# First load swapped, section entered and left through GpSimd, in a batched product of two transposed matrices

## The chip, the cores and the metric

One core of one Trainium2 chip. The metric is the time of one execution in microseconds, on the device. Most executions of a kernel agree within 0.3%. Verdicts use a border of 2%: faster, same, slower. A core has TensorE (PE; PEld is its weight load), VectorE (DVE), ScalarE (ACT), GpSimd (POOL) and SyncE (SP), and 16 transfer (DMA) engines. A span in a profile is shorter than the time of the same execution: 123.0 us against 124.78 us.

## The reference

```python
batch, m, k, n = 16, 512, 512, 512
a: (batch, k, m) float32      b: (batch, n, k) float32
out = np.matmul(a.transpose(0, 2, 1), b.transpose(0, 2, 1))   # float32
```

Both operands come transposed. 16.8 MB of a and of b are read and 16.8 MB written, 50.33 MB in all.

## The kernel before

The batches are loaded whole. Four buffers hold one batch of a each (1.05 MB, 8 KB in each of 128 partitions), three hold a pair of batches of b each (2.10 MB, 16 KB a partition). ScalarE casts a to bf16. VectorE casts b, TensorE turns it against the identity, VectorE copies it back, then TensorE multiplies. SyncE issues all loads from a single queue, in a fixed order, and the last stores; ScalarE issues the first five stores.

```python
with tc.tile_critical():                       # the section; SyncE opens it
    ...
    def run_sp(sp):
        for i in range(B):
            for p in ([0] if i == 0 else [(i + 1) // 2] if i % 2 and i + 1 < B else []):
                if p >= PAIRS:
                    sp.wait_ge(turned, p - PAIRS + 1)
                sp.dma_start(b_sb[p % PAIRS][:], b_v[p]).then_inc(b_in[p % PAIRS], 16)
            s, use = i % LOADS, i // LOADS
            if use:
                sp.wait_ge(summed, MO * (i - LOADS) + 1)    # the buffer has been used
            ...
            sp.dma_start(a_sb[s][:], a_v[i]).then_inc(a_in[s], 16)
        ...                                    # the last stores
        sp.reg_mov(all_stored, 16 * STORED)
    def run_act(act):
        cast_a(act, 0)
        for i in range(B - 1):
            cast_a(act, i + 1)
            copy_out(act, i, slice(2, 4), oa_go)
            j, odd = divmod(i - LAG, 2)
            if odd and 0 <= j < H - TAIL:
                store(act, j)
    ...
nc.sync.wait_ge(stored, nc.sync.snap(all_stored))   # behind the section
```

The first seven loads (10.5 MB) need no wait. They go out at once in the order b0, a0, b1, a1, a2, b2, a3, where b0 is the first pair.

Of the kernel before, what the change touches and what calls it, by code (L numbers as in the profile page):

```python
# [11 lines left out]
def kernel(  # L12
# [6 lines left out]
    nc = tc.nc  # L19
# [15 lines left out]
    a_v = a.rearrange("b (ki ko) m -> b ki ko m", ko=KO)  # L35
# [9 lines left out]
    STORED = H - (H - OUTS) + 1  # L45

    stored = tc.alloc_semaphore("stored")

    all_stored = nc.sync.alloc_register("all_stored")

    with tc.tile_critical():  # L51
        sb = lambda name, shape, dt: ctx.enter_context(nc.sbuf_tensor(name, shape, dt))
        ps = lambda name, shape, dt: ctx.enter_context(nc.psum_tensor(name, shape, dt))
        sem = tc.alloc_semaphore
        a_sb = [sb(f"a_sb{s}", [P, KO, M], f32) for s in range(LOADS)]
# [12 lines left out]
        a_in = [sem(f"a_in{s}") for s in range(LOADS)]  # L68
# [14 lines left out]
        def store(eng, j, part=slice(0, 2)):  # L83


            eng.dma_start(
                out_v[2 * j + part.start:2 * j + part.stop].rearrange("b p mo n -> p b mo n"),
                o_sb[j % OUTS][:, part],
            ).then_inc(o_out[j % OUTS] if j + OUTS < H else stored, 16)

        def run_sp(sp):
            for i in range(B):

                for p in ([0] if i == 0 else [(i + 1) // 2] if i % 2 and i + 1 < B else []):
                    if p >= PAIRS:
# [4 lines that stand above are left out]
                    sp.wait_ge(summed, MO * (i - LOADS) + 1)  # L100
                if i % 2 == 0 and i // 2 >= OUTS:

                    sp.wait_ge(o_out[i // 2 % OUTS], 16 * (i // 2 // OUTS))
                sp.dma_start(a_sb[s][:], a_v[i]).then_inc(a_in[s], 16)

            for j in range(H - TAIL, H - 1):
                sp.wait_ge(summed, MO * (2 * j + 2) + 3)
                store(sp, j)

            sp.wait_ge(summed, MO * (B - 1) + 1)  # L110
            sp.wait_ge(half_go, 1)
            store(sp, H - 1, slice(0, 1))
            sp.wait_ge(last_go, 3)
            store(sp, H - 1, slice(1, 2))
            sp.reg_mov(all_stored, 16 * STORED)

        def run_pool(pool):
            pool.sem_inc(od_go, 1)
            pool.sem_inc(oa_go, 1)
            pool.memset(identity[:], 0.0).then_inc(id_go, 1)  # L120
            pool.wait_ge(id_go, 1)
            pool.affine_select(  # L122
                out=identity[:],
                in_=identity[:],
                compare_op=mybir.AluOpType.not_equal,
                fill=1.0,
                base=0,
                pattern=[[-1, P]],
                channel_multiplier=1,
            ).then_inc(id_go, 1)  # L130

        def cast_a(act, i):
            s = i % LOADS
            act.wait_ge(a_in[s], 16 * (i // LOADS + 1))
            act.copy(a_bf[i % 2][:], a_sb[s][:]).then_inc(ac_go, 1)  # L135
# [56 lines left out]
        def run_pe(pe):  # L192
# [41 lines left out]
            with pe.Fori(0, H) as _i:  # L234
# [6 lines left out]
                half(1, 1)  # L241

        run_sp(nc.sync)
        run_pool(nc.gpsimd)
        run_dve(nc.vector)
        run_act(nc.scalar)
        run_pe(nc.tensor)


    nc.sync.wait_ge(stored, nc.sync.snap(all_stored))  # L250


# [28 lines left out]
```

## Time and profile before

| | before |
|---|---|
| time, median of 3 runs | 124.80 us (124.68 to 124.91) |
| span of the profile | 123.0 us |
| moved | 50.33 MB, 409 GB/s over the span, 427 in its middle |
| first bytes move, last bytes moved | 1.96 us, 121.46 us |
| first product begins | 15.55 us |
| last store asked for, landed | 116.54 us, 121.93 us |

### The profile page before, as it was taken

The numbers are of one execution on the slowest core, as the hardware profiler recorded it, in microseconds if no ns is written. First come the engines' busy times: TensorE is split into PE (matmuls) and PEld (weight loads), VectorE is DVE, ScalarE is ACT, GpSimd is POOL, SyncE is SP. The second block draws the span as 40 slices with busy tenths as digits, with TensorE's granted clock in tenths as the row PEclk, the third lists the DMA queues.
The fourth block names the chain that finished last, engine by engine and source line by source line (L and its number), as shares of the span: only waits on it lengthen the run. The fifth ranks groups of instructions, "written<-read, shape, count | busy, mean of one in ns | idle before, by whom it ended". The sixth has DMA issues, their size and how long they took to land. (4 is left out here: it accounts for less than half of the span.)

```text
span 123.0 us, 1086 instructions
## 1 busy us (share of the span) xinstructions
PE 86.1 (70%) x400; PEld 49.7 (40%) x400; DVE 56.4 (46%) x48; ACT 46.8 (38%) x34; POOL 0.7 (1%) x6
## 2 busy tenths in 40 slices
PE   0006497997999799779930799965992679979600
PEld 0006344642755464346410546442640526437300
DVE  0016368478295755917039107780719306171200
ACT  4003209537717903176300950329230490750300
POOL 2000000000000000000000000000000000000000
PEclk9999999999999999999995557999999558999995
DMA  4999999999999999999999999999999999999992
GB/s 91 394 400 458 400 424 456 429 394 456 426 397 448 434 376 432 426 440 440 416 421 429 458 408 418 429 426 437 453 397 432 426 426 426 429 426 426 429 424 115
DMA packets 5648, 50.33 MB, mean 409 GB/s; under 512 B 528, under 2 KB 528, under 8 KB 528
## 3 DMA queue, kind: packets, MB, share of 16 engines
q1 hardware_dynamic: 4288, 39.85, 77.2%
q10 hardware_dynamic: 1360, 10.49, 20.1%
HBM read 33.55 MB, written 16.78 MB: 409 GB/s over the span
## 5 line engine op out<-in xcount | busy, mean ns | idle before, releaser
L219 PE MATMUL o_ps<-bt_sb,a_bf 128*128 128x512 bf16 x256 | 65.1, 403 | 7.1 <-PEq L194 6.6
L135 ACT CAST a_bf<-a_sb 128x2048 bf16<-128x2048 f32 x16 | 30.4, 1900 | 40.8 <-DMA a_sb<-in_a_dram 40.8
L219 PEld LDWEIGHTS o_ps<-bt_sb,a_bf 128*128 128x128 bf16 x256 | 28.5, 115 | 37.5 <-issue 15.0
L205 PE MATMUL bt_ps<-identity,b_bf 128*128 128x128 f32 x144 | 24.3, 323 | 22.7 <-PEq L194 22.7
L144 DVE COPY o_sb<-o_ps 128x1024 f32<-128x1024 f32 x16 | 19.6, 1224 | 35.8 <-PE o_ps L219 35.8
L205 PEld LDWEIGHTS bt_ps<-identity,b_bf 128*128 128x128 f32 x144 | 22.2, 212 | 28.2 <-issue 27.2
L152 DVE CAST b_bf<-b_sb 128x2048 bf16<-128x2048 f32 x16 | 19.5, 1221 | 19.1 <-DMA b_sb<-in_b_dram 19.1
L144 ACT COPY o_sb<-o_ps 128x1024 f32<-128x1024 f32 (+1 forms) x17 | 16.4, 962 | 28.0 <-PE o_ps L219 28.0
L161 DVE COPY bt_sb<-bt_ps 128x1024 f32<-128x1024 f32 x16 | 19.5, 1216 | 3.1 <-PE bt_ps L205 3.1
L135 ACT ACT_TABLE_LOAD x1 | 1.3, 1283 | 0.9 <-SPq L51 0.9
L122 POOL TENSOR_SCALAR_AFFINE_SELECT identity<-identity 128x128 f32<-128x128 f32 x1 | 0.3, 294 | 0.2 <-POOL identity L120 0.2
L120 POOL MEMSET identity<- 128x128 f32 x1 | 0.2, 205 | 0.7 <-SPq L51 0.7
L265 POOL MEMSET const-bfloat16-1.0<- 128x1 bf16 x1 | 0.1, 102 | 0.0
L265 POOL MEMSET const-uint8-127<- 128x1 uint8 x1 | 0.1, 102 | 0.0
L265 POOL MEMSET const-float32-0.0<- 128x1 f32 x1 | 0.1, 99 | 0.2 <-issue 0.2
L265 POOL MEMSET const-float32-1.0<- 128x1 f32 x1 | 0.1, 99 | 0.0
## 6 DMA issues: line engine op xcount, KB each, us to landing
b_sb<-in_b_dram SPq DMA_DIRECT2D x8, 2048.0 KB, 20.4
a_sb<-in_a_dram SPq DMA_DIRECT2D x16, 1024.0 KB, 17.5
out_dram<-o_sb ACTq DMA_DIRECT2D x5, 2048.0 KB, 15.2
out_dram<-o_sb SPq DMA_DIRECT2D x2, 2048.0 KB, 13.6
out_dram<-o_sb SPq DMA_DIRECT2D x2, 1024.0 KB, 6.3
```

The source lines that it names most:

```text
L120: pool.memset(identity[:], 0.0).then_inc(id_go, 1)
L122: pool.affine_select(out=identity[:], in_=identity[:], compare_op=mybir.AluOpType.not_equal, fill=1.0, base=0, pattern=[[-1, P]], channel_ ...
L135: act.copy(a_bf[i % 2][:], a_sb[s][:]).then_inc(ac_go, 1)
L144: copy(o_sb[i // 2 % OUTS][:, i % 2, rm, :], o_ps[h][:, p, :]).then_inc(go, 1)
L152: dve.tensor_copy(b_bf[:, r, :], b_sb[p % PAIRS][:, r, :]).then_inc(bc_go, n)
L161: dve.tensor_copy(bt_sb[g][:].rearrange("p j (ni r) -> p j ni r", r=NR), bt_ps[:].rearrange("p j r (g ni) -> p g j ni r", g=2)[:, g],).the ...
L205: last = pe.transpose(bt_ps[:, j, r, :], w[:, r, j, :], identity[:])
L219: last = pe.matmul(o_ps[h][:, q, :], a_r[:, rk, 2 * h + q, :], bt_h[:, rk // 2, rk % 2, :], start=(rk == 0), stop=(rk == KO - 1),)
L265: nc = _bacc.Bacc("TRN2", target_bir_lowering=False, num_devices=1)
```

## The change

The intent was to have the first a in hand early, and to start and end a little sooner by letting GpSimd, which already gathers the engines at the barriers of the program, open the section and wait for the last stores.

```diff
-    all_stored = nc.sync.alloc_register("all_stored")
-    with tc.tile_critical():
+    all_stored = nc.gpsimd.alloc_register("all_stored")
+    with tc.tile_critical(sync_engine=nc.gpsimd.engine):
 ...
         def run_sp(sp):
             for i in range(B):
+                if i == 0:
+                    sp.dma_start(a_sb[0][:], a_v[0]).then_inc(a_in[0], 16)
 ...
-                sp.dma_start(a_sb[s][:], a_v[i]).then_inc(a_in[s], 16)
+                if i:
+                    sp.dma_start(a_sb[s][:], a_v[i]).then_inc(a_in[s], 16)
 ...
-            sp.reg_mov(all_stored, 16 * STORED)
         def run_pool(pool):
 ...
+            pool.reg_mov(all_stored, 16 * STORED)
 ...
-    nc.sync.wait_ge(stored, nc.sync.snap(all_stored))
+    nc.gpsimd.wait_ge(stored, nc.gpsimd.snap(all_stored))
```

## The prediction

> **What bounds the kernel now.** I read the page's slices first, because they show which row is full all the time.
>
> ```profile
> PE   0006497997999799779930799965992679979600
> ...
> DMA  4999999999999999999999999999999999999992
> GB/s 91 394 400 458 400 424 456 429 394 456 426 397 448 434 376 432 426 440 440 416 421 429 458 408 418 429 426 437 453 397 432 426 426 426 429 426 426 429 424 115
> DMA packets 5648, 50.33 MB, mean 409 GB/s; under 512 B 528, under 2 KB 528, under 8 KB 528
> ```
>
> The transfer engines stand at 9 in 38 of 40 slices; only the first slice (3.1 us) and the last have room. TensorE falls to 0 and 3 in the middle of the run while transfers stay full, so it waits for data. 50.33 MB is the least that can be moved: each input read once, the output written once. At the 427 GB/s of the middle of the run that alone takes 50.33 / 0.427 = 117.9 us of the 123.0 us span. About 5 us are left at the two edges, and the change can gain only there.
>
> Second view: the windows table at the edges. Columns: window and length; busy time of PE, weight load, DVE, ACT, POOL with counts; granted clock; transfer share; GB/s.
>
> ```profile
> 1.40:1.80 0.40, 0.00 (x0) 0.00 (x0) 0.00 (x0) 0.40 (x1) 0.26 (x1) 1.00 0.00 0
> 1.80:2.00 0.20, 0.00 (x0) 0.00 (x0) 0.00 (x0) 0.20 (x1) 0.03 (x1) 1.00 1.34 328
> ...
> 120.00:120.50 0.50, 0.00 (x0) 0.00 (x0) 0.00 (x0) 0.00 (x0) 0.00 (x0) 0.50 1.00 426
> 120.50:121.00 0.50, 0.00 (x0) 0.00 (x0) 0.00 (x0) 0.00 (x0) 0.00 (x0) 0.50 0.40 164
> 121.00:121.50 0.50, 0.00 (x0) 0.00 (x0) 0.00 (x0) 0.00 (x0) 0.00 (x0) 0.50 0.08 33
> 121.50:122.00 0.50, 0.00 (x0) 0.00 (x0) 0.00 (x0) 0.00 (x0) 0.00 (x0) 0.50 0.00 0
> ```
>
> Data begin to move just under 2.0 us and stop just under 121.5 us. So the span is about 2.0 us of entry, 119.5 us of transfer (a ramp up and down included) and 1.5 us of ending. Third view: the timeline of the first microseconds, which shows the entry and what the order of the loads sets.
>
> ```profile
> 0.90 1.28 ACT L135 ACT_TABLE_LOAD   x1 [0.90 <-SPq L51]
> 0.95 0.39 SPq L97 DMA_DIRECT2D b_sb<-in_b_dram  x1
> ...
> 1.39 0.42 SPq L104 DMA_DIRECT2D a_sb<-in_a_dram  x1
> ...
> 8.81 2.36 DVE L152 CAST b_bf<-b_sb 128x2048 bf16<-128x2048 f32 x2 [8.81 <-DMA b_sb<-in_b_dram]
> 10.15 3.29 PEld L205 LDWEIGHTS bt_ps<-identity,b_bf 128*128 128x128 f32 x16 [10.15 <-issue]
> 10.18 3.61 PE L205 MATMUL bt_ps<-identity,b_bf 128*128 128x128 f32 x16 [10.18 <-PEq L194]
> 11.25 1.90 ACT L135 CAST a_bf<-a_sb 128x2048 bf16<-128x2048 f32 x1 [9.06 <-DMA a_sb<-in_a_dram]
> 13.83 1.23 DVE L161 COPY bt_sb<-bt_ps 128x1024 f32<-128x1024 f32 x1 [2.66 <-PE bt_ps L205]
> ```
>
> Line 51 is the entry of the section: SyncE releases the others there, and itself issues its first load at 0.95 us. The first pair of b is used first: landed at 8.8 us, cast, turned from 10.2 us, copied by 15.06 us. The first a lands at 11.25 us and its cast is done at 13.15 us, some 1.9 us before it could be used.
>
> **What the Trainium skill says.** (1) "DMA: Bandwidth & Descriptors", section "Queues, rings and completion order": on each engine, descriptors of one ring are consumed in order. The trace agrees: b was issued 0.44 us ahead of a, and landed 2.4 us ahead, the time of one a (1.049 MB / 0.427 = 2.46 us). Swapping two loads therefore swaps their turns and adds no bytes. (2) Same page, "Issuing engines are not separate DMA queues": loads and stores from all engines share the same 16 engines, so moving a wait to GpSimd frees no transfer time. The trace agrees: full share throughout, whichever of the two queues is active. (3) "Perfetto Trace Analysis", section on sequencer-only instructions: the wait and the propagation of a semaphore are outside the reported window of such an instruction. In the trace the steps at the ends are spaced some 0.04 to 0.1 us, although each lasts 7 to 50 ns; so I count steps by their spacing. No page I found prices a section entry, and GpSimd issues no DMA in the change.
>
> **The change part by part.**
>
> *First a ahead of first b.* Removed: nothing. Added: nothing. Moved: one 1.049 MB load from second to first place. The first a then lands some 2.5 us after 3.7 us or so, at about 6 us, and its cast is finished by about 8 us, which nobody needs. The b pair lands where a did, near 11.2 us, that is 2.4 us later. From there everything on the path to the first product moves by 2.4 us: casts from 11.2, turning from 12.6, copy from 16.3, first product at about 18.0 us instead of 15.55. The a cast no longer competes, but it never set the start. So this part costs the computation 2.4 us at its head. What does it cost the end? While TensorE is the slower side it carries the delay with it: from 20 to 52 us in the timeline it repeats in about 10.5 us a pair, with gaps under 1 us. Then transfers take over. The wait of DVE for the pair cast at 63.59 us was 5.34 us long, more than twice 2.4, so the delay should be swallowed there. Until then loads are asked for up to 2.4 us later. That drains no queue: no a load took under 9.8 us from issue to landing, of which its own data take 2.5 and its completion about 1, so at least 6 us of other traffic stood ahead of each. Cost to the end: 0.
>
> *Entry through GpSimd.* Of the barrier before the section, GpSimd gathers and then releases: its event steps are at 0.53 and 0.61 us; SyncE wakes at 0.66 and marks the section open at 0.72, and the others then branch at 0.76 to 0.82. With GpSimd as the opener, its mark comes straight after its own release, at about 0.68, and SyncE drops one instruction but waits for GpSimd. I expect its first load at 0.88 to 0.97 instead of 0.95: a gain of 0.04 us, an estimate from the spacing of those steps. The load's start moves the whole transfer train with it.
>
> *The wait for the last stores.* It moves from SyncE to GpSimd. Before: SyncE wakes at 121.95, drains twice at 122.11 and 122.17, GpSimd then gathers at 122.20 and releases at 122.28; the second round ends at 122.9. With the wait on GpSimd the hop from SyncE goes, about 0.06 us; GpSimd's own drain is slower (34 to 99 ns against 7 ns), which gives that back. The register move that leaves SyncE lasted 0.04 us at 116.9 us, 5 us ahead of the landing, so it is hidden anyway. Gain: 0 to 0.1 us, call it 0.05.
>
> Sum: 0 - 0.04 - 0.05 = about -0.1 us. The time is 124.8, so 124.7 us.
>
> **Rivals.** *The late start reaches the end.* The last store is what could show it. In the source view of the stores, the last took 5.4 us from issue to landing; its own 1.049 MB take 2.46 and completion about 1.0, so about 1.9 us of other stores were still ahead of it when it was issued. TensorE may therefore finish up to 1.9 us later at no cost; were all of the 2.4 us to survive, the kernel would lose 0.5 us. If TensorE's half-clock stretches (0.50 in 72 to 74 us, 0.72 mean in 92 to 100 us) fell into the last two batches instead, 1 or 2 us more: 126 to 127. For: the tail has only this 1.9 us. Against: the long waits for data after 60 us.
>
> *A smaller first transfer ramps faster.* In 2.2 to 4.0 us the share is below 1 (0.36 to 1.11) with 2 MB and more queued. If the larger rows of b, 16 KB a partition against 8 KB of a, are the reason, loading a first might win some tenths: 124.4. Against: nothing in the trace tells row size from a cold start, and what follows a is the same b.
>
> *GpSimd is slow to open or to wake.* In the timeline its first instruction of the section stands at 1.11 us against 0.90 on ACT, because two semaphore steps come first. If opening costs it a drain (the 188 ns one at 0.30 us is of that kind), SyncE starts 0.1 to 0.2 us later, and likewise at the end: 125.1.
>
> *Other interleaving.* The first store follows a copy at 40.5 us and moves by 2.4 us, so loads get ahead of stores for a while. With full transfers the order changes no sum; it may move the tail by a few tenths either way.
>
> **Range and chances.** The middle is 124.7. The three runs spread 0.23 us. The edges give -0.25 to +0.3, the ramp -0.3, the tail up to +0.8 in the ordinary case: 124.2 to 125.5 should hold 8 times in 10, with the longer side up because of the tail. A gain over 2% would be 2.5 us, more than the edges could give together without losing necessary steps: 0.01. A loss over 2% needs the throttle in the tail: 0.03. Within 2%: 0.96.
>
> **What would show it.** Right: a lands near 6 us and b near 11.2; the first product starts near 18.0; the transfer row is 9 in the same 38 slices; DVE's wait near 60 us is shorter by about 2.4 us, and later stages stand within 1 us of before; the last store's time from issue to landing stays over 3.5 us; SyncE's first load stands at 0.88 to 0.97, and the ending after the last landing is 1.0 to 1.1 us. Wrong: a slice of the transfer row under 9 before the end; a last store that lands 3.5 us after issue, with no queue ahead of it, and a later end of TensorE; or a first load after 1.1 us.

## The result, and the profile after

| | before | changed |
|---|---|---|
| median of 6 runs each | 124.82 us (124.60 to 125.45) | 124.67 us (124.43 to 124.75) |
| ratio, 95% interval | | 0.9979 (0.9955 to 1.0003) |
| span of the profile | 123.0 us | 123.0 us |
| first product begins | 15.55 us | 17.55 us |
| last store asked for, landed | 116.54, 121.93 us | 114.84, 121.92 us |

A ratio is the mean time of one kernel's runs over that of the other's in the same rounds, so not quite the ratio of the medians. Executions over 1.5% slower than the fastest of the same kernel are left out of the means.

The page of the changed kernel, slices of the span (a digit is the busy share in tenths):

```profile
PE   0000949899889979979996988047999489979100
...
DMA  3999999999999999999999999999999999999992
GB/s 69 442 426 426 410 429 440 429 410 440 426 413 440 426 413 370 450 416 434 416 426 429 445 429 424 424 426 448 421 418 426 424 426 429 426 426 426 426 429 115
DMA packets 5648, 50.33 MB, mean 409 GB/s; under 512 B 528, under 2 KB 528, under 8 KB 528
```

The transfer row is 9 in the same 38 slices. The first two slices moved more than before (69 and 442 against 91 and 394 GB/s; a packet counts in the slice where it starts), the 16th less than its neighbours (370). TensorE starts a slice later. The timeline of the changed kernel's head:

```profile
0.89 0.38 SPq L94 DMA_DIRECT2D a_sb<-in_a_dram  x1
...
5.91 1.90 ACT L139 CAST a_bf<-a_sb 128x2048 bf16<-128x2048 f32 x1 [3.73 <-DMA a_sb<-in_a_dram]
10.76 2.36 DVE L156 CAST b_bf<-b_sb 128x2048 bf16<-128x2048 f32 x2 [10.76 <-DMA b_sb<-in_b_dram]
...
12.13 3.66 PE L209 MATMUL bt_ps<-identity,b_bf 128*128 128x128 f32 x16 [12.13 <-PEq L198]
...
17.55 4.77 PE L223 MATMUL o_ps<-bt_sb,a_bf 128*128 128x512 bf16 x12 [1.76 <-PEq L198]
```

The first load goes out 0.06 us earlier. The first a is cast from 5.91 us (before: 11.25), the first pair of b from 10.76 us (before: 8.81), and the first product begins 2.0 us later.

Where the delay went is seen on VectorE. Its timeline before, then changed; the number in brackets is the idle time in front of an instruction and what ended it:

```profile
63.59 1.23 DVE L152 CAST b_bf<-b_sb 128x2048 bf16<-128x2048 f32 x1 [5.34 <-DMA b_sb<-in_b_dram]
...
77.08 1.23 DVE L152 CAST b_bf<-b_sb 128x2048 bf16<-128x2048 f32 x1 [0.56 <-DMA b_sb<-in_b_dram]
...
91.73 1.23 DVE L152 CAST b_bf<-b_sb 128x2048 bf16<-128x2048 f32 x1 [2.87 <-DMA b_sb<-in_b_dram]
```

```profile
60.75 1.22 DVE L156 CAST b_bf<-b_sb 128x2048 bf16<-128x2048 f32 x1
...
77.91 1.23 DVE L156 CAST b_bf<-b_sb 128x2048 bf16<-128x2048 f32 x1 [6.13 <-DMA b_sb<-in_b_dram]
...
91.44 1.23 DVE L156 CAST b_bf<-b_sb 128x2048 bf16<-128x2048 f32 x1 [0.42 <-DMA b_sb<-in_b_dram]
```

Before, VectorE waited 5.34 us for a pair of b at 63.6 us. In the changed kernel that pair was there when VectorE came, and the wait of 6.13 us stands one pair later. By 91 us both kernels are back at the time set by the transfers.

The delay grew on the way:

```profile
15.55 3.80 PE L219 MATMUL o_ps<-bt_sb,a_bf 128*128 128x512 bf16 x16 [1.76 <-PEq L194]
20.23 1.20 PE L205 MATMUL bt_ps<-identity,b_bf 128*128 128x128 f32 x8 [0.88 <-PEq L194]
```

```profile
17.55 5.69 PE L223 MATMUL o_ps<-bt_sb,a_bf 128*128 128x512 bf16 x16 [1.76 <-PEq L198]
23.82 1.20 PE L209 MATMUL bt_ps<-identity,b_bf 128*128 128x128 f32 x8 [0.58 <-PEq L198]
```

The first 16 products took 5.69 us instead of 3.80, so TensorE turned the next b 3.6 us later than before, and SyncE asked for an a at 25.96 instead of 22.36 us, also 3.6 us later. The change alone does not do that: in the three profiles of the changed kernel these products took 5.69, 5.12 and 3.81 us. The granted clock was 1.00 in both kernels here; why they differ is not shown.

At the end the changed kernel asks for its last store earlier, so more queue is ahead of it. This is the landing line of the last stores, from the source view, before and then changed:

```profile
DMA to landing us min/median/max: 5.4/7.2/8.6
```

```profile
DMA to landing us min/median/max: 7.1/8.9/10.4
```

TensorE has 1.7 us more room at the tail (7.1 - 5.4), not less, and nothing comes of it: the last store lands at 121.92 instead of 121.93 us.

**The head start that did not last.** From the trace's packets I summed the bytes moved up to a time, cutting packets at that time, and divided the difference to the profile of before by 427 GB/s. At 10 us and at 40 us the changed kernel is 0.3 us ahead. At 50 us it is 0.04 us ahead, and so until the end. The loss falls where the first store begins: it was asked for at 44.05 us, and its first packet moved at 47.8. Against an even 427 GB/s the changed kernel lost 0.39 us of bytes between 40 and 50 us, two thirds of it ahead of that packet; the kernel before lost 0.13 us there. The windows of the changed kernel there (second last column: transfer share; last: GB/s):

```profile
46.00:47.00 1.00, 1.00 (x6) 0.49 (x5) 0.00 (x0) 0.85 (x1) 0.00 (x0) 1.00 1.08 393
47.00:48.00 1.00, 1.00 (x7) 0.68 (x6) 0.06 (x1) 0.00 (x0) 0.00 (x0) 1.00 0.99 320
```

The share stays at 1 while the bytes fall: the 8 KB packets of the loads took up to 0.64 us there instead of 0.309. So a full transfer row does not say that the rate is full.

### The profile page after: what moved, and what is told of

It is laid out like the page before. It is cut to its first block, busy times and chain, and to the rows that moved or that the text cites. A ratio compares the mean times of both kernels' runs of the same rounds, so it can differ in the third digit from the quotient of the medians.

```text
span 123.0 us, 1080 instructions
## 1 busy us (share of the span) xinstructions
PE 85.2 (69%) x392; PEld 49.4 (40%) x400; DVE 56.2 (46%) x48; ACT 46.8 (38%) x34; POOL 0.7 (1%) x6
## 5 line engine op out<-in xcount | busy, mean ns | idle before, releaser
L223 PE MATMUL o_ps<-bt_sb,a_bf 128*128 128x512 bf16 x248 | 63.6, 405 | 5.7 <-PEq L198 4.6
L209 PE MATMUL bt_ps<-identity,b_bf 128*128 128x128 f32 x144 | 23.7, 317 | 23.4 <-PEq L198 23.4
L209 PEld LDWEIGHTS bt_ps<-identity,b_bf 128*128 128x128 f32 x144 | 21.6, 211 | 28.6 <-issue 27.6
```

What stands on the lines that cost most here:

```text
L209: last = pe.transpose(bt_ps[:, j, r, :], w[:, r, j, :], identity[:])
L223: last = pe.matmul(o_ps[h][:, q, :], a_r[:, rk, 2 * h + q, :], bt_h[:, rk // 2, rk % 2, :], start=(rk == 0), stop=(rk == KO - 1),)
```

## The experiments

Eleven kernels ran, in three groups; each group ran on one chip and shared its runs of before (median 125.00, 124.96 and 124.77 us). Three questions: which part of the change gives the small gain; whether a later head costs nothing, and up to what delay; and why the head start is lost. The theories are the prediction's (transfers bound the time, edges alone count), and against it "a later head reaches the end".

### The order alone

```diff
 (kernel before)
+                if i == 0:
+                    sp.dma_start(a_sb[0][:], a_v[0]).then_inc(a_in[0], 16)
-                sp.dma_start(a_sb[s][:], a_v[i]).then_inc(a_in[s], 16)
+                if i:
+                    sp.dma_start(a_sb[s][:], a_v[i]).then_inc(a_in[s], 16)
```

> Only the order: the first a ahead of the first b, section entered and left through SyncE as before. Theory 'ramp' (the changed kernel's 0.3 us of head start in bytes moved comes from its 8 KB rows going first): first load issued at 0.95 us, no bytes gained or lost by the entry, but about 0.2 us more moved by 10 us than before (3.02 MB then, 3.12 here), first product near 17.6 us; time 0.0 to 0.25 us under before. Theory 'entry' (the head start is the earlier issue of the first load): no more bytes by 10 us than before, time equal to before within 0.1 us. Both: no cost at the end of the 2 us later first product.

Measured: 124.78 us, ratio 0.9986 (0.9967 to 1.0005). First load at 0.95 us, first product at 17.75 us. Bytes by 10 us: 0.16 us ahead of before, as the ramp theory expected, with no earlier issue. After its first store it was 0.30 us behind before. So the order gives a head start of its own, and it does not keep it.

### The entry and the last wait alone

```diff
 (changed kernel)
-                if i == 0:
-                    sp.dma_start(a_sb[0][:], a_v[0]).then_inc(a_in[0], 16)
-                if i:
-                    sp.dma_start(a_sb[s][:], a_v[i]).then_inc(a_in[s], 16)
+                sp.dma_start(a_sb[s][:], a_v[i]).then_inc(a_in[s], 16)
```

> Only the entry and the last wait through GpSimd, b first as before. Theory 'entry': first load issued at 0.89 us instead of 0.95, ending 0.02 us shorter, so 0.05 to 0.1 us less time and 0.06 us more bytes moved at 10 us; first product at 15.5 us. Theory 'ramp': the same 0.06 us, and the further 0.2 us of the changed kernel missing. Rival 'GpSimd is slow': 0.1 to 0.3 us more than before.

Measured: 124.79 us, ratio 0.9983 (0.9964 to 1.0003). First load at 0.89 us, first product at 15.39 us, 0.08 us ahead by 10 us and still 0.06 us at 110 us. GpSimd woke at 122.03 us and the last instruction began at 122.99, 0.97 us later; before, SyncE woke at 121.95 and it began at 122.93, 0.98 us later. The entry gives what its steps said; the ending gives 0.02 us at most; GpSimd is not slow. Its traced gain is smaller than its timed one of 0.2 us, whose interval includes none; its span in the profile, 123.04 us, was not shorter than before (122.99).

### The first pair of b as two halves

```diff
 (entry alone)
+                    if p == 0:
+                        sp.dma_start(b_sb[0][:, :NR // 2], b_v[0][:, :NR // 2]).then_inc(b_half, 16)
+                        sp.dma_start(b_sb[0][:, NR // 2:], b_v[0][:, NR // 2:]).then_inc(b_in[0], 16)
+                        continue
 (the cast of the first half waits for b_half)
```

> Entry through GpSimd, b first, but its first pair loaded as two transfers of half the rows each: 8 KB a partition, 1.05 MB, like a. Theory 'ramp by row size': the same head start in bytes at 10 us as the changed kernel (3.14 MB, 0.3 us over before), though b goes first; first product near 13.7 us, some 3.8 us earlier than in the changed kernel; time equal to the changed kernel within 0.2 us, because the transfers bound it. Rival 'it is something of b': head start no larger than with the entry alone (0.06 us). Rival 'computation at the head counts': 2 to 4 us less time than the changed kernel.

Measured: 124.97 us, ratio 1.0005 (0.9985 to 1.0024). By 10 us it was 0.23 us ahead, 0.15 more than with the entry alone, although b went first. So the smaller transfer with 8 KB a partition ramps faster, and nothing of b holds it back. Its size and its row were halved together, so which of them counts is open. The first 16 packets took 0.7 to 1.9 us with 16 KB before (0.611 us each later on), and 0.5 to 1.3 us with 8 KB in the changed kernel (0.309 us later on). The head start was gone by 46 us (0.07 us behind). The first product began at 13.77 us, 3.8 us before the changed kernel's, and the time was not shorter but 0.36 us longer (1.0005 / 0.9976 of the next run, in the same rounds, times 124.6; the means of their six runs are 124.95 and 124.61 us). That falsifies "the computation at the head counts"; my "within 0.2 us" was too narrow.

### The changed kernel again, twice

> The changed kernel as it is, in the same rounds as the parts: 0.1 to 0.35 us under before. If the parts add up, its gain is that of order alone plus that of entry alone within 0.15 us. Its profile shows a head start of 0.3 us in bytes by 10 us again, if that is no accident of one execution; whether the dip to about 370 GB/s in the slice at 46 to 49 us comes again, just ahead of the first store's first packets, is open.

Measured: 124.59 us, ratio 0.9976 (0.9956 to 0.9996). Ahead by 0.27 us at 10 us and by 0.00 us at 50 us. The dip came again, ahead of its first store's first packet at 47.4 us. The sum of the two parts' gains is 0.0031, this one 0.0024: they add up within the error, which here is as large as each part.

> The changed kernel a third time, as the control of these rounds: 0.1 to 0.4 us under before (ratio 0.997 to 0.999). Both theories expect the same here.

Measured, in the last group: 124.64 us, ratio 0.9984 (0.9970 to 0.9997). The head start was 0.41 us at 10 us, the loss at the first store 0.59 us. Three sets of runs thus put the gain at 0.2 to 0.3 us (0.0016 to 0.0024 of 125; by the medians 0.15, 0.41 and 0.13 us), two of the three intervals clear of none. The loss at the first store, 0.25, 0.27 and 0.59 us for one and the same kernel, shows how far single profiles may be trusted.

### More a loads ahead of the first b

With two, three and four in place of one; the loop then leaves those out:

```diff
 (changed kernel)
                 if i == 0:
-                    sp.dma_start(a_sb[0][:], a_v[0]).then_inc(a_in[0], 16)
+                    for n in range(4):                       # or 2, 3
+                        sp.dma_start(a_sb[n][:], a_v[n]).then_inc(a_in[n], 16)
-                if i:
+                if i >= 4:                                   # or 2, 3
```

> The smallest dose of a later head: two a loads ahead of the first b, first product 2.5 us later than in the changed kernel, near 20.0 us. With one (the changed kernel) nothing was lost, with three 1.2 us, with four 3.9 us. Theory 'the queue ahead of each load swallows it, and it runs dry on single engines before it does in sum': nothing to 0.4 us over the changed kernel (124.6 to 125.1), no slice of the transfer row under 380 GB/s other than the one at the first store. Rival 'each microsecond of head beyond the changed kernel costs': 0.6 us or more (125.2 or over).

> The changed kernel with three a loads (3.15 MB) ahead of the first b: the first product 4.9 us later than in the changed kernel, near 22.4 us, 6.9 us later than before. Theory 'transfers bound it, the head is swallowed': a load asked for at 30.8 us in the changed kernel landed 9.5 us later, of which 2.5 are its own data and about 1 its start and completion, so some 6 us of queue stood ahead of it; 4.9 us more delay leaves about 1 us: time equal to the changed kernel within 0.3 us (124.4 to 125.0). Rival 'a later head reaches the end': 3 to 5 us more.

> Four a loads ahead of the first b: the first product 7.4 us later than in the changed kernel, near 24.9 us. Theory 'swallowed by the queue': now the delay exceeds the 6 us of queue, so the transfer row shows a gap of 1 to 2.5 us between 35 and 52 us and the time rises by just that, 1.0 to 2.5 us (125.6 to 127.2). Rival 'a later head reaches the end': 6 to 7.4 us more. Rival 'swallowed by waits of TensorE for data, whatever the queue': no change.

| a loads ahead of the first b | first product | least left in SyncE's queue | time | ratio, 95% interval |
|---|---|---|---|---|
| 0 (entry alone) | 15.39 us | 3.6 MB | 124.79 us | 0.9983 (0.9964 to 1.0003) |
| 1 (changed kernel again) | 17.47 us | 2.6 MB | 124.59 us | 0.9976 (0.9956 to 0.9996) |
| 2 | 19.93 us | 2.1 MB | 124.72 us | 0.9993 (0.9977 to 1.0008) |
| 3 | 22.40 us | 1.0 MB | 124.80, 125.97 and 126.32 us; 127.41 left out as slow | 1.0034 (0.9986 to 1.0082) |
| 4 | 24.60 us | 0.7 MB | 128.57 us | 1.0294 (1.0267 to 1.0320) |

The third column is what was still to move of SyncE's earlier transfers when it asked for its next load, at the worst moment up to 50 us (asked for, less the bytes moved in the trace). The run of 127.41 us counts as slow by its time alone; its clock, 0.943, was that of the others. With three, then, the time scatters by 2.6 us.

So 2 to 4.5 us of later head cost nothing that these runs can tell, and 9.2 us (24.60 - 15.39) cost 3.9 us (1.0294 - 0.9983 of 125). The rival "a later head reaches the end" is false for the small doses. My size was off for the large ones: I had read the queue ahead of a load as some 6 us in sum and expected the loss to begin only with four, at 1.0 to 2.5 us. The kernel with four, in windows, and then the changed kernel in the same ones:

```profile
20.00:30.00 10.00, 7.37 (x37) 5.15 (x36) 6.17 (x6) 1.56 (x2) 0.00 (x0) 1.00 0.94 374
30.00:40.00 10.00, 9.06 (x45) 5.00 (x45) 6.45 (x7) 5.09 (x5) 0.00 (x0) 1.00 0.96 396
40.00:50.00 10.00, 9.42 (x48) 5.32 (x47) 6.43 (x7) 5.08 (x4) 0.00 (x0) 1.00 0.99 397
50.00:60.00 10.00, 9.57 (x48) 5.52 (x48) 6.45 (x7) 5.15 (x4) 0.00 (x0) 1.00 1.01 391
```

```profile
20.00:30.00 10.00, 9.28 (x44) 5.19 (x44) 6.62 (x6) 3.21 (x4) 0.00 (x0) 1.00 1.01 426
30.00:40.00 10.00, 9.06 (x47) 5.29 (x46) 6.45 (x7) 5.26 (x4) 0.00 (x0) 1.00 1.00 419
40.00:50.00 10.00, 8.98 (x46) 5.43 (x47) 6.44 (x6) 5.63 (x4) 0.00 (x0) 1.00 1.01 409
50.00:60.00 10.00, 8.98 (x46) 5.28 (x46) 6.44 (x7) 5.63 (x4) 0.00 (x0) 1.00 1.01 428
```

In these windows of 10 us the rate with four is down from 20 to 60 us, by 12 to 52 GB/s, and looks like one long stretch. Shorter windows show that it is not:

```profile
20.00:27.00 7.00, 5.24 (x26) 3.93 (x25) 3.17 (x4) 0.00 (x0) 0.00 (x0) 1.00 0.98 417
27.00:29.00 2.00, 1.40 (x7) 0.46 (x4) 2.00 (x3) 0.56 (x1) 0.00 (x0) 1.00 0.82 221
29.00:37.00 8.00, 7.65 (x41) 4.78 (x42) 4.60 (x4) 4.16 (x4) 0.00 (x0) 1.00 1.00 418
37.00:42.00 5.00, 4.13 (x23) 2.40 (x22) 3.49 (x3) 3.72 (x3) 0.00 (x0) 1.00 0.91 346
42.00:48.00 6.00, 5.93 (x31) 3.37 (x30) 3.79 (x4) 2.36 (x2) 0.00 (x0) 1.00 1.00 422
48.00:54.00 6.00, 5.13 (x30) 3.37 (x29) 3.78 (x4) 3.27 (x3) 0.00 (x0) 1.00 1.04 362
```

I had expected one gap, between 35 and 52 us. There are three dips, which cost 0.9, 1.0 and 1.1 us of bytes, and between them the rate is nearly full. Each begins about 1 us after a load that was asked for with under 1 MB left in SyncE's queue: 0.66 MB at 25.70 us, 0.80 at 36.24, 0.92 at 46.78. With three a loads the least was 1.03 MB, at 44.57 us, and from 47 to 48 us the share was 0.83 and the rate 336 GB/s. So loads came too late for a queue that in sum still held 1.5 to 2.4 us of data (0.66 to 1.03 MB at 427 GB/s). That single engines run dry first would fit, but is argued: the 16 engines' completions of one load lay 0.3 us apart up to 28 us, and 1.8 to 2.8 us apart from the first reload (landed at 32.2 us) to 60 us. The third dip runs into the loss at the first store (asked for at 49.53 us): from 51 us the share is 1 again and packets take longer. Why they do is not shown.

### The first store on the other queue

```diff
 (changed kernel)
                 if i:
                     sp.dma_start(a_sb[s][:], a_v[i]).then_inc(a_in[s], 16)
+                if i == 8:
+                    sp.wait_ge(summed, MO * 2 + 3)
+                    store(sp, 0)
-                if odd and 0 <= j < H - TAIL:
+                if odd and 0 < j < H - TAIL:
```

> The changed kernel with the first store alone issued through SyncE's queue instead of ACT's. Open is why the 0.3 us head start in bytes disappears between 44 and 50 us. Theory 'the first use of ACT's queue slows the running loads': no dip under 400 GB/s between 42 and 54 us at this store, the head start of 0.27 us over before lives until the next store, which is then the first on ACT's queue, and is lost there (near 55 us): time equal to the changed kernel. Theory 'the first write to memory does it': the dip comes where this store's data begin, whatever the queue. Theory 'chance': no dip anywhere, 0.3 us less.

Measured: 124.81 us, ratio 0.9984 (0.9964 to 1.0004). The head start of 0.27 us survived to 46 us. It fell to 0.18 us between 48 and 50 us, where this store began on SyncE's queue, and to -0.02 us between 55 and 60 us, where ACT's queue was used first. So in this one profile neither theory holds alone: each start took about half. Chance is out as the cause of the dip, which came in every profile of the changed kernel; the halves themselves are rough.

### ACT's queue used at the start

```diff
 (changed kernel)
-                if i == 0:
-                    sp.dma_start(a_sb[0][:], a_v[0]).then_inc(a_in[0], 16)
         def run_act(act):
+            act.dma_start(a_sb[0][:], a_v[0]).then_inc(a_in[0], 16)
```

> The changed kernel with its first a issued through ACT's queue at the start, beside the first b on SyncE's. Theory 'the first use of ACT's queue slows the running loads': that use is now at the start, so no dip under 400 GB/s near the first store at 42 to 48 us, and the head start survives to the end: 0.2 to 0.4 us under the changed kernel, unless the start itself loses as much. Theory 'the first write to memory': the dip at the first store stays, time equal to the changed kernel within 0.1 us. The first product near 15.5 to 17 us in both.

Measured: 124.59 us, ratio 0.9974 (0.9953 to 0.9995), first product at 17.92 us. The head start at 10 us was only 0.13 us; two queues shared the start (the first b and a landed at 11.10 and 11.29 us). But it lived: 0.21 us at 50 us and 0.22 us at 110 us. In the time it does not show: I had expected 0.2 to 0.4 us under the changed kernel, whose ratio in the other rounds was 0.9976 to 0.9984. In the profile the last store landed at 121.69 us, against 121.83 to 121.94 in the changed kernel's three. The same windows at the first store, this kernel and then the changed one:

```profile
46.00:48.00 2.00, 2.00 (x12) 1.17 (x10) 0.01 (x1) 0.91 (x1) 0.00 (x0) 1.00 1.06 438
```

```profile
46.00:48.00 2.00, 2.00 (x12) 1.18 (x11) 0.06 (x1) 0.85 (x1) 0.00 (x0) 1.00 1.03 356
```

The dip is gone, which speaks for the first use of the queue. But the kernel before also uses ACT's queue first at its first store, and lost little there: its packets from 43 to 45 us took 0.14 us an engine more than 0.309 or 0.611 us each, in the changed kernel from 46 to 48 us it was 0.38 us. So the first use is not enough as a cause. A short queue is not the cause either: at 46 us 3.6 MB were left in SyncE's queue in this kernel and in the changed one alike.

### Halves of b on two queues

```diff
 (the first pair as two halves)
-                        sp.dma_start(b_sb[0][:, NR // 2:], b_v[0][:, NR // 2:]).then_inc(b_in[0], 16)
         def run_act(act):
+            act.dma_start(b_sb[0][:, NR // 2:], b_v[0][:, NR // 2:]).then_inc(b_in[0], 16)
```

> The best of the parts in one kernel: entry and last wait through GpSimd, the first pair of b as two halves with 8 KB a partition, one on SyncE's queue and one on ACT's, then a on SyncE's. First product near 13.7 us. Theory 'head starts are lost at the first use of ACT's queue': that use is at the start here, so the head start (0.2 to 0.3 us of bytes by 10 us) reaches the end: 0.1 to 0.3 us under the changed kernel run in the same rounds, a span of 122.6 to 122.7. Theory 'the slowest of the 16 engines sets the end, and it is the same whatever the start': the spread of the engines' completions is about 1 us again by the last store, and the time equals the changed kernel's within 0.1 us.

Measured: 124.66 us, ratio 0.9990 (0.9976 to 1.0004), against 0.9984 for the changed kernel in the same rounds. The first product began at 15.19 us, not 13.7, because the halves shared the start: they landed at 8.4 and 9.0 us, and one after the other on one queue at 6.2 and 8.7. The head start was 0.06 us at 10 us and 0.01 us at 110 us: nothing much to lose, little lost (0.16 us from 40 to 50 us, against 0.13 before). So the theory that a head start reaches the end when ACT's queue is used at the start got no test here. No version beat the changed kernel beyond the noise.

**What stays open.** Kernels with 16 KB rows at the head lose little at the first store; those with 8 KB rows on one queue lose 0.3 to 0.6 us more there than before, unless ACT's queue was used at the start; with the first store on SyncE's queue it came in two parts. The engines' spread changes at the same place: in the changed kernel the first and the last engine's completions of a load lay 0.45 us apart until the first store and 0.96 us after, before they lay 1.07 us apart from the start, and both ended with about 1 us (1.11 and 0.98). This would fit an end that is set by the slowest engine, with the leaders held up at the first store. Other profiles speak against it as the whole cause: with b in halves on one queue the engines were 0.91 us apart ahead of the store, and it still lost 0.3 us more than before; and the changed kernel's other two profiles ended 0.84 and 0.62 us apart. No run tested it by itself, and the cause stays open.

## Why the prediction was right

- **Transfers bound it, and 5 us at the edges are all there is.** Right. The transfer row kept its 38 slices, and a head 3.8 us earlier or 2.5 us later than the changed kernel's moved the time by 0.4 us or less.
- **First a ahead of first b: computation later, end unmoved.** Right. It said first a near 6 us, first b near 11.2, first product near 18.0; measured 5.88, 10.74 and 17.55. All came up to 0.5 us earlier; 0.3 us of it is the head start in bytes.
- **Swallowed at VectorE's long wait near 60 us.** Right in kind, one pair early in place: that wait vanished, and the shift, by then 2.6 us (VectorE's last copy ahead of it at 59.62 instead of 57.04 us), was carried on until the wait of 6.13 us at 77.9 us. Later stages were to stand within 1 us of before; some did (77.91 for 77.08, 91.44 for 91.73 us), the last store was asked for 1.7 us earlier.
- **Loads asked for up to 2.4 us later, at least 6 us of queue ahead of each.** Both sizes were off, and the conclusion held with room. The loads were asked for up to 3.6 us later. The 9.8 us belong to the first a, asked for at the start; the quickest reload took 14.3 us (16.66 to 30.97). And the "about 1" for completion is 0.5 us from the last byte to the landing, with 1.0 us from the issue to the first byte on top (0.95 to 1.96), so the reload had some 10 us of queue ahead of it (an estimate, 14.3 - 2.5 - 1.5). A sum in us is the wrong measure of the slack all the same: the rate already dipped with 1.0 MB, 2.4 us, left.
- **Entry through GpSimd, -0.04 us.** Right: the first load at 0.89 instead of 0.95 us, -0.06 us.
- **Last wait on GpSimd, -0.05 us.** Right in sign, smaller: 0.01 to 0.02 us.
- **The rival "a smaller first transfer ramps faster".** It happened, with 0.15 us of bytes where some tenths were given for it, and the sum had put it at 0. It did not reach the end, since the first store took it back. The rival had no such step, and neither had I.
- **"With full transfers the order changes no sum" (the rival on interleaving).** Wrong: at the first store, 3.6 us later than before, 0.39 us of bytes were lost with the transfer share at 1, against 0.13 us before.
- **The tail with its 1.9 us.** Not needed: the last store had 1.7 us more ahead of it than before.
- **The sum.** -0.1 us was predicted, -0.2 to -0.3 us was timed in three sets, inside the range. The two profiles account for less than that: their spans differ by under 0.1 us. Which part the timed rest belongs to is not settled; each part alone gave about 0.2 us, and each interval includes no gain at all. That the number came out so near is in part luck: the ramp was priced at 0, and so was its loss.

## What to carry to other kernels

Where the transfers are full from end to end, reordering the first loads moves the computation and not the end; read the slack from how long a load waits in the queue, and take well under the sum: here the rate dipped with 0.7 to 1.0 MB, 1.5 to 2.4 us, still to move. A gain at the head counts only if it is still there at the end: compare bytes moved at several times, not just the first landings. Look at GB/s beside the busy share, as the share stayed near 1 while the rate fell to 320. Take short windows: in windows of 10 us, three dips looked like one slow stretch.

## What the Trainium skill lacked or had wrong

- "DMA: Bandwidth & Descriptors", section "Where 436 GB/s comes from", says that for transfers between HBM and SBUF the HBM side (about 358 GB/s) binds. Here one core alone moved 427 to 428 GB/s from 60 to 120 us. The same page's measured table, which says that it is for one core with the other idle, has 425 and agrees.
- The same page gives the ramp of a transfer by its size, for GpSimd's path only. No page has what the first transfer of a program costs by the bytes a partition: 0.15 us of head start for 8 KB against 16 KB here, the first 16 packets 0.5 to 1.3 and 0.7 to 1.9 us against 0.309 and 0.611 us later on.
- No page has the loss at a first store: from 40 to 50 us 0.13 us of bytes before, 0.39, 0.39 and 0.72 us in the changed kernel's three profiles, and 0.04 and 0.16 us in the two kernels whose storing queue had carried a load at the start.
- No page prices opening a section or its last wait by engine: first load at 0.95 us through SyncE and 0.89 us through GpSimd, and the ending 0.01 to 0.02 us shorter through GpSimd.
